# A two-layer decoder on one core: what is pinned behind a layer norm, the first pairs turned together, and other rates for the conditioning vectors

## The chip, the cores and the metric

The kernel runs on one core of a Trainium2 chip. The metric is the time of one execution on the device in microseconds. Before the change it is 2311.81 us, the median of three runs. A core has five engines that run side by side and wait for each other through semaphores: TensorE (PE, with its weight loads as PEld), VectorE (DVE), ScalarE (ACT), GpSimd (POOL) and SyncE (SP), which here issues the loads of weights.

## The reference

Two layers over 256 rows of width 2048, all in float32. Every sub-layer is `x <- LayerNorm(alpha * x + (1 + gate) * F(x * (1 + scale) + shift))`; shift, scale and gate come from a conditioning vector c through a 2048 x 12288 matrix per layer.

```python
c_act = silu(c)
for i in range(2):
    sh1, sc1, g1, sh2, sc2, g2 = split(c_act @ ada_w[i] + ada_b[i], 6)
    h = x * (1 + sc1) + sh1
    y = fox_attention(h) if i == 0 else swa_attention(h, positions)
    x = layer_norm(ALPHA * x + (1 + g1) * y)
    h = x * (1 + sc2) + sh2
    y = conv_ffn(h)                # up 2048 -> 2*5632, conv of width 3, silu gate, down
    x = layer_norm(ALPHA * x + (1 + g2) * y)
```

`fox_attention` has 16 heads of 128 with a forgetting term; `swa_attention` has 32 query heads of 64, 4 key/value heads, a window of 128, sinks and partial rotary.

## The kernel before

**Matrix products.** Everything is in float32 precision made of two parts: a value is split into a rounded high part (`h`) and a residual (`l`), and a product takes high x high, high x low and low x high. Weights come in tiles of 256 x 512 (`wtile`, 512 KB, ten buffers shared with the loads below). `stream` handles each tile: SyncE loads it (L265), ScalarE makes the high part (`wh`, L268), VectorE the residual (`wl`, L281), each with four buffers, and the function `go` runs the tile's matmuls: first all that need `wh`, then those that need `wl`. The modulated activations stand transposed in `hHL`, high and low parts, 16 chunks of 128 columns; a tile uses two chunks, called a pair here. `x_mm` keeps the rows of x as weights of TensorE (attention projections, down projections), `w_stationary` the weight tile (up projections of the FFN).

**Order of the work.** The program is written out in full by Python, and a planner then orders the instructions of each engine: by the order in which they were written, but an instruction that its model takes to be ready earlier may go ahead of one that is not. `pin` takes that freedom from an instruction: it is put behind the instruction written just before it on its engine. `work` is a queue of tiles (`go`) and small functions; `settle` runs it so that two tiles stay ahead, and `rest` writes the residuals (L281) of the next tiles before the current one runs, up to three in all. While `feeds` is not empty, `rest` writes only one.

**Layer norms.** There are three norms inside the program: behind the forgetting attention (near 489 us), behind the first FFN (near 1250 us) and behind the window attention (near 1543 us). The last `residual` adds the sub-layer to x and gathers statistics by halves of 128 rows (L573 to L587). A `halt` then calls `between`, which calls `modulate`. It runs ten matmuls on constants (`warm`), and eight feeds, one for each pair. A feed normalises a quarter of x where it begins one (`normalise`: rows 0 to 127 on ScalarE, L597; the others on VectorE, L599), transposes the pair on TensorE (`mod_turn`, L459), and applies scale and shift (`mod_pair`). The first two pairs take the fast form: for each chunk ScalarE writes the high part from PSUM (L469), VectorE computes the whole value from the same PSUM bank (L470) and subtracts (L471). The other six use L473 and L474 for a chunk each, then L85 and L86. Two feeds run at once, and each of the following six tiles runs one at its end. All of it is pinned, and so are the residuals of the tiles that were streamed while the halt was waiting or feeds were left.

**Conditioning vectors.** Ten of the twelve vectors are computed in the shadow of other work: `ada_vector` loads 32 parts of 512 KB, each with one VectorE operation (L396, the first of each half L394), and then needs some small matmuls and an evacuation, 37 steps in all. `ada_tick` runs after every tile: it adds `rate` to a debt and makes one step for each whole unit. `ada_need` makes what is missing at once where a vector is needed: the third norm needs the vectors that are written up to there. Functions put in `work` change the rate by stage. The first FFN has 96 and 80 tiles of up projections and 48 and 40 of down projections, in turn; the window attention 8 tiles for keys and values, 32 for queries, 32 for the output.

Of the kernel before, what the change touches and what calls it, by code (L numbers as in the profile page):

```python
# [17 lines left out]
P = 128  # L18
# [23 lines left out]
def hybrid_trunk(ctx: ExitStack, tc: tile.TileContext, a: dict, out: bass.AP):  # L42
# [23 lines left out]
    def bank(name="sm"):  # L66
        return psp.tile([P, 512], F32, tag="ps", name=name)
# [10 lines left out]
    def pin(ins, on=True):  # L78

        if on:  # L80
            tc.keep_in_program_order(ins)

    def split(h, l, src, on=False):

        pin(nc.scalar.copy(h, src), on)  # L85
        pin(nc.vector.tensor_tensor(l, src, f32(h), op=ALU.subtract), on)  # L86

    def split_v(h, l, src):
        nc.vector.tensor_copy(h, src)
# [134 lines left out]
    def rest(*items):  # L224

        n = 0
        for f in items:
            if f in stops:
                return
            if f in residuals:  # L230
                residuals[f]()
                n += 1
                if feeds:
                    return
            elif f in weights:
                n += 1
            if n > 2 - (items[0] not in weights):
                return
# [3 lines left out]
        stops.add(fn)  # L242
        then(fn)

    residuals, weights, stops = {}, set(), set()

    def defer(gen):

# [7 lines left out]
    def flush():  # L256
        while post:
            run_post()

    def stream(wsrc, row0, col, ks, use):  # L260

        for kc in ks[::2]:
            r0 = (row0 + kc) * P
            w = wtile()
            pin(nc.sync.dma_start(w, wsrc[r0:r0 + 2 * P, col:col + WB].rearrange("(k p) f -> p k f", p=P)), False)  # L265
            h = hl.tile([P, 2, WB], F32R, tag="wh", name="wh")
            l = hl.tile([P, 2, WB], F32R, tag="wl", name="wl")
            pin(nc.scalar.copy(h, w), False)  # L268

            def go(kc=kc, h=h, l=l):  # L270
                ahead[0] -= 1
                run_post()
                use(kc, h, l)
                if feeds:
                    feeds.pop(0)()
                tick()

            behind = bool(feeds) or any(f in stops for f in work)

            def residual_(w=w, h=h, l=l, go=go, behind=behind):  # L280
                pin(nc.vector.tensor_tensor(l, w, f32(h), op=ALU.subtract), behind or feeds)  # L281
                del residuals[go]

            ahead[0] += 1
            weights.add(go)
            residuals[go] = residual_
            work.append(go)
            settle(2)

    def x_mm(ps, kc, h, l, stat, last, first=0, ts=range(NT)):  # L290

        for t in ts:
            for i in range(2):
                xh, xl = stat(kc + i, t)
                mm(ps[t], xh, h[:, i, :], start=kc + i == first)
                mm(ps[t], xl, h[:, i, :])
        for t in ts:
            for i in range(2):
                mm(ps[t], stat(kc + i, t)[0], l[:, i, :], stop=kc + i == last)
# [33 lines left out]
    def w_stationary(wsrc, col):  # L333

        ps = [bank("wd") for _ in range(4)]

        def use(kc, h, l):
            cells = [(i, f) for i in range(2) for f in range(4)]
            for i, f in cells:
                mm(ps[f], h[:, i, f * P:(f + 1) * P], hHL[:, kc + i].rearrange("p a s -> p (a s)"),  # L340
                   start=kc + i == 0)
            for i, f in cells:
# [117 lines left out]
            os.append(o)  # L460
        return os

    def mod_pair(G, B, k, ps, fast=False, on=False):
        tmp = ttile()
        if fast:
            for j in range(2):
                o = tmp[:, j * S:(j + 1) * S]
                g, b = G[:, k + j:k + j + 1], B[:, k + j:k + j + 1]
                pin(nc.scalar.activation(hH[:, k + j, :], ps[j], AF.Identity, bias=b, scale=g))  # L469
                pin(nc.vector.tensor_scalar(o, ps[j], g, b, op0=ALU.mult, op1=ALU.add))  # L470
                pin(nc.vector.tensor_tensor(hL[:, k + j, :], o, f32(hH[:, k + j, :]), op=ALU.subtract))  # L471
            return
        pin(nc.scalar.activation(tmp[:, :S], ps[0], AF.Identity, bias=B[:, k:k + 1], scale=G[:, k:k + 1]), on)  # L473
        pin(nc.vector.tensor_scalar(tmp[:, S:], ps[1], G[:, k + 1:k + 2], B[:, k + 1:k + 2],  # L474
                                    op0=ALU.mult, op1=ALU.add), on)
        split(hH[:, k:k + 2, :], hL[:, k:k + 2, :], tmp.rearrange("p (j s) -> p j s", j=2), on)

    def hstat(kc, t):
        return hH[:, kc, t * P:(t + 1) * P], hL[:, kc, t * P:(t + 1) * P]
# [87 lines left out]
    moments = [None] * NT  # L567

    def residual(ps, d, gate, last):
        for t in range(NT):  # L570
            tmp = ttile()
            end = last and d == D // 512 - 1
            pin(nc.vector.tensor_tensor(tmp, ps[t], gate[:, d * 512:(d + 1) * 512], op=ALU.mult), end)  # L573
            xs = x[:, t, d * 512:(d + 1) * 512]
            pin(nc.vector.tensor_tensor(xs, xs, tmp, op=ALU.add), end)  # L575
            if last:
                pin(nc.vector.bn_stats(stats[:, t, d, :], xs), end)  # L577
                if d == D // 512 - 1:
                    mv = sp.tile([P, 2], F32, tag="mv", name="mv")
                    pin(nc.vector.bn_aggr(mv, stats[:, t].rearrange("p a b -> p (a b)")))  # L580
                    rs = sp.tile([P, 2], F32, tag="rs", name="rs")
                    pin(nc.vector.tensor_scalar_add(rs[:, 0:1], mv[:, 1:2], EPS))  # L582
                    if t == 0:
                        pin(nc.vector.tensor_scalar_mul(rs[:, 1:2], mv[:, 0:1], -1.0))
                    nc.gpsimd.tensor_tensor(rs[:, 0:1], rs[:, 0:1], mhalf, op=ALU.pow)
                    if t == 0:
                        nc.scalar.mul(rs[:, 1:2], rs[:, 1:2], rs[:, 0:1])  # L587
                    moments[t] = (mv[:, 0:1], rs[:, 0:1], rs[:, 1:2])
            yield

    def normalise(d):

        for t in range(NT):
            mu, rs, nm = moments[t]
            xs = x[:, t, d * 512:(d + 1) * 512]
            if t == 0:
                pin(nc.scalar.activation(xs, xs, AF.Identity, scale=rs, bias=nm))  # L597
            else:
                pin(nc.vector.tensor_scalar(xs, xs, mu, rs, op0=ALU.subtract, op1=ALU.mult))  # L599

# [86 lines left out]
    def out_proj(oT, full, w_o, l):  # L687
        def stat(kc, t):
            while kc not in full:
                step()  # L690
            return oT[kc][0][:, t * P:(t + 1) * P], oT[kc][1][:, t * P:(t + 1) * P]

        ps = {d: x_banks() for d in range(2)}

        def part(d, ks):
            use = x_mm_end(ps[d], stat, KC, 2) if d == D // WB - 1 else                 lambda kc, h, l_: x_mm(ps[d], kc, h, l_, stat, KC - 1)
            stream(w_o, 0, d * WB, ks, use)

        for i, ks in enumerate((range(0, 8), range(8, 12))):
            then(lambda i=i: ada.update(rate=((1.4,1.4,1.8,1.8), (1.05,)*4)[l][i]))  # L700
            for d in range(2):
                part(d, list(ks))
        then(lambda: ada_need(l, 2))
        for d in range(D // WB):
            if d < 2:
                part(d, list(range(12, KC)))
            else:
                then(lambda d=d: ada.update(rate=((1.4,1.4,1.8,1.8), (1.05,)*4)[l][d]))
# [202 lines left out]
    def swa(l, j):  # L911
# [94 lines left out]
    def conv_ffn(l):  # L1006
# [42 lines left out]
        for si, (b0, b1) in enumerate(sbs):  # L1049
# [79 lines left out]
```

## Time and profile before

| | |
|---|---|
| median of three runs | 2311.81 us |
| the profiled execution | 2310.31 us |
| its span, first to last instruction | 2308.4 us |
| TensorE busy | 2226.6 us, 96% of the span |
| VectorE busy | 1866.2 us, 81% |
| ScalarE busy | 1184.0 us, 51% |
| moved by DMA | 602.68 MB, mean 261 GB/s |
| L281, residuals of weights | 728 times, 1222 ns each |
| L396, conditioning vectors | 300 times, 1279 ns each |

A row of the timeline gives the start, the length, the engine, the line, the operation, what is written and read, how many were merged, and in square brackets how long the engine was idle before it and which instruction ended that. "xs", "wd" and "ws" are PSUM tiles of products, "sm" and "warm" small PSUM tiles. A row of busy time by stretch gives the busy time of each engine, the clock that TensorE was granted as a share of full speed, the busy share of the DMA engines and the bytes moved.

### The profile page before, as it was taken

What the parts mean: (1) busy time and instruction counts of PE and PEld (TensorE: products, weight loads), DVE (VectorE), ACT (ScalarE), POOL (GpSimd) and SP (SyncE); (2) the same over time, 40 slices, a digit from 0 to 9 for tenths busy, and PEclk for the clock granted to TensorE, in tenths of its full rate; (3) what the DMA queues carried; (4) which work ended last, traced back from release to release, by engine and by line L of the source; (5) the groups of instructions that cost most, each with busy time, mean ns of one, the idle gap of its engine ahead of it and who ended that gap; (6) DMA issues with size and microseconds to landing.
All of it is one profiled execution on the core that took longest, in us unless ns stands there. A gap on an engine that the chain in (4) does not pass through costs nothing. (4 is left out here: it accounts for less than half of the span.)

```text
span 2308.4 us, 33416 instructions
## 1 busy us (share of the span) xinstructions
PE 2226.6 (96%) x12225; PEld 1905.8 (83%) x12225; DVE 1866.2 (81%) x2783; ACT 1184.0 (51%) x1859; POOL 66.7 (3%) x83
## 2 busy tenths in 40 slices
PE   7889999999999999999999999998999999999997
PEld 7779898777888888888887777777888888888886
DVE  6898998969988886897986898888988754667666
ACT  3335644445655533555634478735665533555542
POOL 3230000000000000000000000000000000000000
PEclk9999999999999999999999999999999999999999
DMA  9998999958987897887896785787888556666553
GB/s 342 328 337 279 352 354 355 323 199 277 323 276 235 293 319 241 279 291 237 270 316 222 247 296 199 257 293 238 297 266 266 179 194 193 191 191 192 187 195 111
DMA packets 285989, 602.68 MB, mean 261 GB/s; under 512 B 20790, under 2 KB 53752, under 8 KB 285312
## 3 DMA queue, kind: packets, MB, share of 16 engines
q1 hardware_dynamic: 284768, 595.85, 76.9%
q0 software_dynamic: 1056, 4.69, 0.6%
q8 instruction: 96, 1.57, 0.3%
q14 instruction: 69, 0.57, 0.1%
HBM read 598.37 MB, written 2.10 MB: 260 GB/s over the span
## 5 line engine op out<-in xcount | busy, mean ns | idle before, releaser
L268 ACT CAST wh<-w 128x1024 fp32r<-128x1024 f32 x728 | 763.2, 1051 | 768.9 <-PE xs L76 263.5
L281 DVE TENSOR_TENSOR wl<-w,wh 128x1024 fp32r<-128x1024 f32 x728 | 887.7, 1222 | 306.3 <-ACT wh L268 285.5
L76 PE MATMUL wd<-hHL,wh 128*128 128x512 f32 x2816 | 720.3, 398 | 6.7 <-DVE hHL L86 3.3
L76 PEld LDWEIGHTS wd<-hHL,wh 128*128 128x128 f32 x2816 | 505.1, 189 | 108.3 <-DVE hHL L86 5.3
L76 PEld LDWEIGHTS wd<-hHL,wl 128*128 128x128 f32 x2816 | 374.3, 188 | 40.4 <-DVE wl L281 9.2
L76 PE MATMUL wd<-hHL,wl 128*128 128x256 f32 x2816 | 381.6, 278 | 6.3 <-DVE wl L281 6.2
L396 DVE SCALAR_TENSOR_TENSOR acc<-wa,cact,acc 128x1024 f32<-128x1024 f32 x300 | 380.7, 1279 | 0.0
L76 PE MATMUL xs<-wh,gT 128*128 128x512 f32 x1408 | 349.4, 389 | 0.0
L76 PEld LDWEIGHTS xs<-wh,gT 128*128 128x128 f32 x1408 | 263.6, 188 | 54.4
L76 PE MATMUL xs<-wl,gT 128*128 128x512 f32 x704 | 189.2, 389 | 0.0
L76 PE MATMUL xs<-wh,hHL 128*128 128x512 f32 x704 | 184.8, 399 | 3.4 <-DVE hHL L86 2.4
L76 PEld LDWEIGHTS xs<-wl,gT 128*128 128x128 f32 x704 | 132.1, 188 | 27.5
L76 PE MATMUL ws<-hHL,wh 128*128 128x256 f32 x1024 | 136.5, 287 | 16.1 <-ACT wh L268 16.1
L76 PEld LDWEIGHTS xs<-wh,hHL 128*128 128x128 f32 x704 | 127.8, 189 | 28.4 <-DVE hHL L86 2.7
L76 PEld LDWEIGHTS ws<-hHL,wh 128*128 128x128 f32 x1024 | 127.2, 193 | 21.9 <-ACT wh L268 21.3
L1019 ACT ACTIVATE u<-s,ccol 128x256 f32<-128x256 f32 x176 | 105.1, 600 | 65.0 <-DVE s L1014 50.3
L76 PE MATMUL xs<-wl,hHL 128*128 128x512 f32 x352 | 98.3, 399 | 4.1 <-DVE wl L281 4.1
L76 PE MATMUL xs<-wh,oT 128*128 128x512 f32 x384 | 99.1, 396 | 1.5 <-ACT wh L268 1.3
L528 DVE SCALAR_TENSOR_TENSOR oacc<-wo,cact,oacc 128x256 f32<-128x256 f32 x212 | 92.0, 494 | 6.2 <-POOL oacc L526 6.2
L1020 DVE SCALAR_TENSOR_TENSOR u<-s,ccol,u 128x255 f32<-128x255 f32 x176 | 84.4, 480 | 6.7 <-ACT u L1019 6.4
L1022 DVE SCALAR_TENSOR_TENSOR u<-s,ccol,u 128x254 f32<-128x254 f32 x176 | 84.1, 478 | 1.2
L76 PEld LDWEIGHTS xs<-wh,oT 128*128 128x128 f32 x384 | 70.7, 190 | 15.9 <-ACT wh L268 1.7
(218 smaller groups left out, 1705.3 us busy)
## 6 DMA issues: line engine op xcount, KB each, us to landing
w<-in_ffn_w_up_dram SPq DMA_DIRECT2D x352, 512.0 KB, 4.6
wa<-in_ada_w_dram SPq DMA_DIRECT2D x320, 512.0 KB, 4.9
w<-in_ffn_w_down_dram SPq DMA_DIRECT2D x176, 512.0 KB, 4.4
w<-in_fox_w_in_dram SPq DMA_DIRECT2D x96, 512.0 KB, 5.6
wo<-in_ada_w_dram SPq DMA_DIRECT2D x64, 512.0 KB, 6.4
w<-in_swa_w_in_dram SPq DMA_DIRECT2D x40, 512.0 KB, 4.8
w<-in_fox_w_o_dram SPq DMA_DIRECT2D x32, 512.0 KB, 6.0
w<-in_swa_w_o_dram SPq DMA_DIRECT2D x32, 512.0 KB, 5.6
```

The source lines that it names most:

```text
L76: return nc.tensor.matmul(o, lhsT, rhs, start=start, stop=stop, **kw)
L268: pin(nc.scalar.copy(h, w), False)
L281: pin(nc.vector.tensor_tensor(l, w, f32(h), op=ALU.subtract), behind or feeds)
L396: pin(nc.vector.scalar_tensor_tensor(ac, wo, cact[:, k:k + 1], ac, op0=ALU.mult, op1=ALU.add), True)
L528: nc.vector.scalar_tensor_tensor(acc[:, v, k % 2, :], w[:, k, :], cact[:, kc:kc + 1], acc[:, v, k % 2, :], op0=ALU.mult, op1=ALU.add)
L1019: nc.scalar.activation(u, s, AF.Identity, bias=cw(CW, f), scale=cw(2, f))
L1020: nc.vector.scalar_tensor_tensor(u[:, 1:], s[:, :S - 1], cw(1, f), u[:, 1:], op0=ALU.mult, op1=ALU.add)
L1022: nc.vector.scalar_tensor_tensor(u[:, 2:], s[:, :S - 2], cw(0, f), u[:, 2:], op0=ALU.mult, op1=ALU.add)
```

## The change

Six edits go together.

1. `mod_pair`: only the fast form's VectorE operations stay pinned. The other six pairs, ScalarE's part of `normalise` and ScalarE's L469 are left to the planner.
2. `rest` and `stream`: only the first two tiles streamed behind a halt have their residuals pinned and written one at a time (`behind`). Later tiles have them written up to three ahead, unpinned, while feeds are left.
3. `modulate`: the first quarter is normalised first; both first pairs are transposed together, all of rows 0 to 127, then six warming matmuls, then all of rows 128 to 255, then four. The warming matmuls stay twenty in all.
4. `mod_pair`, fast form: ScalarE takes chunk 0 while VectorE takes chunk 1, then the other way round; then the two subtractions.
5. `feed`: the next pair is turned in the middle of a tile, between the matmuls on `wh` and those on `wl`, not at its end.
6. Rates: window attention 1.25 to 0.95 (queries) and 1.05 to 0.9 (output); down projections of the first FFN 0.6 to 0.8.

In `residual` the same instructions are only written in another arrangement of the code.

```diff
     def rest(*items):
...
-                if feeds:
+                if f in behind:
                     return
...
+    fed = [False]
+
+    def feed():
+
+        if feeds and not fed[0]:
+            fed[0] = True
+            feeds.pop(0)()
...
                 run_post()
+                fed[0] = False
                 use(kc, h, l)
-                if feeds:
-                    feeds.pop(0)()
+                feed()
                 tick()
 
-            behind = bool(feeds) or any(f in stops for f in work)
-
-            def residual_(w=w, h=h, l=l, go=go, behind=behind):
-                pin(nc.vector.tensor_tensor(l, w, f32(h), op=ALU.subtract), behind or feeds)
+            def residual_(w=w, h=h, l=l, go=go):
+                pin(nc.vector.tensor_tensor(l, w, f32(h), op=ALU.subtract), go in behind)
                 del residuals[go]
 
+            if any(f in stops for f in work) and sum(f in behind for f in work) < 2:
+                behind.add(go)
...
                 mm(ps[t], xl, h[:, i, :])
+        feed()
         for t in ts:
...
-    def mod_pair(G, B, k, ps, fast=False, on=False):
+    def mod_pair(G, B, k, ps, fast=False):
         tmp = ttile()
         if fast:
+            g, b = ([c[:, k + j:k + j + 1] for j in range(2)] for c in (G, B))
+            o = [tmp[:, j * S:(j + 1) * S] for j in range(2)]
+            high = lambda j: nc.scalar.activation(hH[:, k + j, :], ps[j], AF.Identity, bias=b[j], scale=g[j])
+            whole = lambda j: pin(nc.vector.tensor_scalar(o[j], ps[j], g[j], b[j], op0=ALU.mult, op1=ALU.add))
+            high(0), whole(1), high(1), whole(0)
             for j in range(2):
-                o = tmp[:, j * S:(j + 1) * S]
-                g, b = G[:, k + j:k + j + 1], B[:, k + j:k + j + 1]
-                pin(nc.scalar.activation(hH[:, k + j, :], ps[j], AF.Identity, bias=b, scale=g))
-                pin(nc.vector.tensor_scalar(o, ps[j], g, b, op0=ALU.mult, op1=ALU.add))
-                pin(nc.vector.tensor_tensor(hL[:, k + j, :], o, f32(hH[:, k + j, :]), op=ALU.subtract))
+                pin(nc.vector.tensor_tensor(hL[:, k + j, :], o[j], f32(hH[:, k + j, :]), op=ALU.subtract))
             return
...
     def modulate(G, B, norm):
 
+        norm(0)
         warm(10)
-
-        def feed(k):
+        ps = {k: [bank() for _ in range(2)] for k in (0, 2)}
+        for t in range(NT):
+            for k in ps:
+                for j in range(2):
+                    pin(nc.tensor.transpose(ps[k][j][:, t * P:(t + 1) * P], x[:, t, (k + j) * P:(k + j + 1) * P], ident))
+            warm(6 - 2 * t)
+        for k in ps:
+            mod_pair(G, B, k, [b[:, :S] for b in ps[k]], True)
+
+        def feed_(k):
             if k % 4 == 0:
                 norm(k // 4)
-            o = mod_turn(k, 2)
-            if k < 4:
-                warm(5)
-            mod_pair(G, B, k, o, k < 4, True)
-
-        feeds.extend([lambda k=k: feed(k) for k in range(0, KC, 2)])
-        for _ in range(2):
-            feeds.pop(0)()
+            mod_pair(G, B, k, mod_turn(k, 2))
+
+        feeds.extend([lambda k=k: feed_(k) for k in range(4, KC, 2)])
...
     def normalise(d):
...
-                pin(nc.scalar.activation(xs, xs, AF.Identity, scale=rs, bias=nm))
+                nc.scalar.activation(xs, xs, AF.Identity, scale=rs, bias=nm)
...
-            then(lambda i=i: ada.update(rate=((1.4,1.4,1.8,1.8), (1.05,)*4)[l][i]))
+            then(lambda i=i: ada.update(rate=((1.4,1.4,1.8,1.8), (0.9,)*4)[l][i]))
...
-        then(lambda: ada.update(rate=1.25))
+        then(lambda: ada.update(rate=.95))
...
-                ada["rate"] = (0.6, 0.4)[l]
+                ada["rate"] = (0.8, 0.4)[l]
```

More of the change, by code (lines that the diff above doesn't have):

```diff
@@ L81, in pin, with split @@
             tc.keep_in_program_order(ins)
-    def split(h, l, src, on=False):
-        pin(nc.scalar.copy(h, src), on)
-        pin(nc.vector.tensor_tensor(l, src, f32(h), op=ALU.subtract), on)
+    def split(h, l, src):
+        nc.scalar.copy(h, src)
+        nc.vector.tensor_tensor(l, src, f32(h), op=ALU.subtract)
     def split_v(h, l, src):
@@ L243, in halt @@
         then(fn)
-    residuals, weights, stops = {}, set(), set()
+    residuals, weights, stops, behind = {}, set(), set(), set()
     def defer(gen):
@@ L341, in use @@
                    start=kc + i == 0)
+            feed()
             for i, f in cells:
@@ L569, in residual @@
     def residual(ps, d, gate, last):
+        c0 = d * 512
+        end = last and d == D // 512 - 1
         for t in range(NT):
             tmp = ttile()
-            end = last and d == D // 512 - 1
-            pin(nc.vector.tensor_tensor(tmp, ps[t], gate[:, d * 512:(d + 1) * 512], op=ALU.mult), end)
-            xs = x[:, t, d * 512:(d + 1) * 512]
+            xs = x[:, t, c0:c0 + 512]
+            pin(nc.vector.tensor_tensor(tmp, ps[t], gate[:, c0:c0 + 512], op=ALU.mult), end)
             pin(nc.vector.tensor_tensor(xs, xs, tmp, op=ALU.add), end)
@@ L577, in residual @@
                 pin(nc.vector.bn_stats(stats[:, t, d, :], xs), end)
[L578 to L588, printed above, removed]
+            if end:
+                mv = sp.tile([P, 2], F32, tag="mv", name="mv")
+                pin(nc.vector.bn_aggr(mv, stats[:, t].rearrange("p a b -> p (a b)")))
+                rs = sp.tile([P, 2], F32, tag="rs", name="rs")
+                pin(nc.vector.tensor_scalar_add(rs[:, 0:1], mv[:, 1:2], EPS))
+                if t == 0:
+                    pin(nc.vector.tensor_scalar_mul(rs[:, 1:2], mv[:, 0:1], -1.0))
+                nc.gpsimd.tensor_tensor(rs[:, 0:1], rs[:, 0:1], mhalf, op=ALU.pow)
+                if t == 0:
+                    nc.scalar.mul(rs[:, 1:2], rs[:, 1:2], rs[:, 0:1])
+                moments[t] = (mv[:, 0:1], rs[:, 0:1], rs[:, 1:2])
             yield
@@ L707, in out_proj @@
             else:
-                then(lambda d=d: ada.update(rate=((1.4,1.4,1.8,1.8), (1.05,)*4)[l][d]))
+                then(lambda d=d: ada.update(rate=((1.4,1.4,1.8,1.8), (0.9,)*4)[l][d]))
                 ps[d] = x_banks()
```

8 lines of the change are left out of this document (4 added, 4 removed).

## The prediction

> **What bounds the kernel now.** I read the page's busy times first, then busy time by stage, then the timeline behind the first layer norm, then who waited for whom.
>
> ```profile
> PE 2226.6 (96%) x12225; PEld 1905.8 (83%) x12225; DVE 1866.2 (81%) x2783; ACT 1184.0 (51%) x1859; POOL 66.7 (3%) x83
> ```
>
> TensorE is busy for 96% of 2308.4 us, so only its 82 us of idle time, plus matmuls that fill a wait, can be won. Columns below: stretch, its length, busy us of PE, PEld, DVE, ACT, POOL, granted clock, DMA share, GB/s.
>
> ```profile
> 0.00:170.00 170.00, 142.50 (x950) 129.90 (x950) 134.69 (x265) 60.16 (x76) 50.66 (x57) 0.99 0.99 336
> 498.50:521.00 22.50, 20.60 (x117) 17.03 (x118) 15.38 (x22) 12.48 (x18) 0.00 (x0) 1.00 0.61 187
> 521.00:561.00 40.00, 35.28 (x189) 29.16 (x188) 39.16 (x52) 21.20 (x30) 0.00 (x0) 0.96 0.83 275
> 552.00:555.00 3.00, 0.53 (x6) 0.34 (x4) 3.00 (x5) 1.27 (x4) 0.00 (x0) 0.93 0.87 289
> 555.00:559.00 4.00, 4.00 (x16) 3.59 (x17) 4.00 (x5) 0.99 (x1) 0.00 (x0) 0.63 1.00 348
> 770.00:900.00 130.00, 130.00 (x605) 108.58 (x604) 96.94 (x104) 53.42 (x60) 0.00 (x0) 1.00 0.81 281
> 1125.00:1246.00 121.00, 121.00 (x562) 101.08 (x561) 100.72 (x112) 52.12 (x59) 0.00 (x0) 1.00 0.87 303
> 1259.00:1283.00 24.00, 21.96 (x110) 17.15 (x109) 14.56 (x21) 14.14 (x20) 0.00 (x0) 1.00 0.41 119
> 1283.00:1400.00 117.00, 110.13 (x557) 88.87 (x556) 113.16 (x235) 75.44 (x174) 3.26 (x4) 1.00 0.82 282
> 1400.00:1538.00 138.00, 134.50 (x674) 109.95 (x673) 122.12 (x240) 91.78 (x217) 0.00 (x0) 1.00 0.75 261
> 1552.50:1575.00 22.50, 19.99 (x114) 16.34 (x114) 14.46 (x22) 13.25 (x19) 0.00 (x0) 1.00 0.58 184
> 1575.00:1616.00 41.00, 37.12 (x197) 31.03 (x198) 38.87 (x55) 20.34 (x31) 0.00 (x0) 0.96 0.81 261
> ```
>
> Three places lose time. While pairs are turned behind a norm (498.5, 1259, 1552.5) TensorE idles 1.90 + 2.04 + 2.51 = 6.45 us though VectorE is idle too (7.12, 9.44, 8.04 us): order, not work, is the limit. In the 40 us after that in each FFN, VectorE is full (39.16 of 40, 38.87 of 41) and TensorE idles 4.72 and 3.88 us. In the window attention's query projection VectorE is full again (113.16 of 117) and TensorE idles 6.87 us. The FFN's down projections (770, 1125) are the contrast: TensorE never idles and VectorE has 33.06 and 20.28 us free.
>
> **The gap at a norm.** The timeline behind the first norm:
>
> ```profile
> 488.30 0.63 PE L76 MATMUL xs<-wl,hHL 128*128 128x512 f32 x2
> 488.76 2.44 PE L76 MATMUL warm<-ones 128*128 128x512 f32 x10
> 492.89 0.44 PE L459 MATMUL sm<-ident,x 128*128 128x128 f32 x2 [1.48 <-DVE x L599]
> 493.26 1.02 ACT L469 ACTIVATE hHL<-sm,B,G 128x256 fp32r<-128x256 f32 x2 [2.58 <-PE sm L459]
> 493.86 0.55 DVE L470 TENSOR_SCALAR t<-sm,G,B 128x256 f32<-128x256 f32 x1 [1.02 <-ACT hHL L469]
> 494.44 0.42 DVE L471 TENSOR_TENSOR hHL<-t,hHL 128x256 fp32r<-128x256 f32 x1
> 495.92 2.02 PE L76 MATMUL wd<-hHL,wh 128*128 128x512 f32 x8
> 497.53 2.35 DVE L281 TENSOR_TENSOR wl<-w,wh 128x1024 fp32r<-128x1024 f32 x2
> 498.80 0.39 PE L76 MATMUL wd<-hHL,wl 128*128 128x256 f32 x1 [0.43 <-DVE wl L281]
> ```
>
> The last matmul ends at 488.93; the next useful one starts at 495.92. Up to 492.89 the path is the second half's statistics, which the change leaves alone. Then VectorE's L470 waits for ScalarE's L469 although both only read the same bank. With the engines on different banks VectorE starts with ScalarE at 493.26 instead of 493.86. Its eight operations are in order, so the first residual (497.53) and the matmuls on it (498.80) come 0.6 us earlier. The first matmul at 495.92 could come 0.97 earlier (493.26, two L470 of 0.55, an L471 of 0.42 and the handing over: the pair's first half is ready near 494.95), but the residual is late next, so I take 0.6 each, 1.8 for three; bounds 0.4 (six warming matmuls at 2.44 / 10 last 1.46 us and end just when the transposes are due) and 0.97.
>
> **Pairs in mid-tile, only the chain pinned.** Further on in the same stretch:
>
> ```profile
> 507.67 0.54 DVE L599 TENSOR_SCALAR x<-x,mv,rs 128x512 f32<-128x512 f32 x1
> 510.90 0.69 DVE L86 TENSOR_TENSOR hHL<-t,hHL 128x512 fp32r<-128x512 f32 x1 [1.60 <-ACT hHL L85]
> 511.64 2.13 PE L76 MATMUL wd<-hHL,wh 128*128 128x512 f32 x8 [0.91 <-DVE hHL L86]
> 517.05 1.05 ACT L268 CAST wh<-w 128x1024 fp32r<-128x1024 f32 x1 [3.16 <-DMA w<-in_ffn_w_up_dram]
> 554.96 2.08 PE L76 MATMUL wd<-hHL,wl 128*128 128x256 f32 x8 [2.47 <-DVE wl L281]
> ```
>
> A pair takes from 507.67 to 511.59 through VectorE, TensorE and ScalarE, and VectorE waits 1.60 us inside it because everything behind is pinned; TensorE waits for the pair at 511.64. Unpinned, VectorE can do a residual of 1.22 us in such a hole, and the pair starts half a tile earlier. No trace shows the new order, so the bounds are 0 and 6.45 us for the three stretches; I take half, 3.2, since part of the idle time is residuals and ScalarE.
>
> In the full stretches after it, VectorE's work is the same; only a head start helps, of up to the two more residuals that the lifted limit in `rest` allows. A residual is
>
> ```profile
> L281 DVE TENSOR_TENSOR wl<-w,wh 128x1024 fp32r<-128x1024 f32 x728 | 887.7, 1222 | 306.3 <-ACT wh L268 285.5
> L396 DVE SCALAR_TENSOR_TENSOR acc<-wa,cact,acc 128x1024 f32<-128x1024 f32 x300 | 380.7, 1279 | 0.0
> ```
>
> so 0 to 2.44 us for each FFN; I take one, 2.4 for both. The stall at 554.96 also costs clock: PE is busy 0.53 of 3 us, and the next 4 us are granted 0.63, so 4 x 0.37 + 3 x 0.07 = 1.7 us more are lost. The other FFN loses 41 x 0.04 = 1.6 the same way. I take one of the two as gone, 1.7; bounds 0 and 3.3. The Trainium skill (TensorE: Matmul & The Clock Gate, "HAM oscillation — how this bites in real kernels") has idle gaps over about 3.4 us as what throttles; by it the 2.47 us wait costs no clock and the whole sum would be 1.7 smaller. The trace disagrees, with 0.63 granted behind that wait.
>
> **The rates.** Each tile pays the rate into a debt; a vector takes 37 steps, 32 of them a load with one VectorE operation. Between the first norm and the third six vectors are due, 222 steps. The tiles are 176 up, 88 down, 8 key/value, 32 query, 32 output: before 176 x 0.52 + 88 x 0.6 + 8 x 0.3 + 32 x 1.25 + 32 x 1.05 = 220.3, so two steps are forced at the third norm; after 91.5 + 70.4 + 2.4 + 30.4 + 28.8 = 223.5, none. Running this count step by step, loads in the query projection go from 34 to 26, in the output projection from 30 to 22, in key/value from 0 to 2, in FFN0's down projections from 24 and 23 to 33 and 27, and one goes into an up projection. The trace bears the count out: between the second norm and the third it has
>
> ```profile
> L396 DVE SCALAR_TENSOR_TENSOR acc<-wa,cact,acc x60: 1260/1279/1287, 1301.0 to 1534.8; 128x1024 f32<-128x1024 f32 x60
> wa<-in_ada_w_dram SPq DMA_DIRECT2D x320, 512.0 KB, 4.9
> ```
>
> 60, which with two first rows for each of two vectors, written in another form, are the 34 + 30.
>
> The query projection loses 8 x 1.28 = 10.2 us of VectorE's 113.16. Its waits on TensorE's side:
>
> ```profile
> PE xs L76 <- DVE wl L281: 2.5, 4, 1.3
> PE qp L962 <- DVE qq L954: 2.5, 4, 1.1
> PE xs L76 <- ACT wh L268: 1.1, 1, 1.1
> ```
>
> 5.0 us are VectorE being late. I take 3.5, bounds 0 and 6.87: the wait at L962 is partly a chain's length. The output projection has VectorE at 122.12 of 138, not full: 0.5, bounds 0 and 3.50. FFN0's 13 more down loads I cost at nothing: 9 x 1.28 = 11.5 lies in 33.06 free, 4 x 1.28 = 5.1 in 20.28. DMA goes from 281 to 281 + 9 x 0.524 MB / 130 us = 317 GB/s, under the 336 at which the first row is full (0.99). Without that cover it is 13 x 1.28 = 16.6 us.
>
> One cover does go: the last vector's column sums sit in the third norm's gap.
>
> ```profile
> 1541.10 1.84 PE L76 MATMUL sm<-ones,acc 128*128 128x1 f32 x16
> 1542.80 2.56 PE L76 MATMUL warm<-ones 128*128 128x512 f32 x10
> ```
>
> Finished earlier, these 1.84 us stand between busy matmuls: +1.8, bounds 0 and 1.84.
>
> **Sum.** -1.8 - 3.2 - 2.4 - 1.7 - 3.5 - 0.5 + 1.8 = -11.3 us. The profiled execution took 2310.31 (2 us around its span), so 2299.0; the median shown is 2311.81, 1.5 more, which gives 2300.5. I say 2300.
>
> **Rivals.**
> - Only the arithmetic edits pay: the new order shifts TensorE's waits behind the norms without shortening them, since VectorE is full by 521 anyway. -1.8 - 3.5 - 0.5 + 1.8 = -4.0, so 2308. For it: 39.16 of 40. Against: 7 to 9 us of VectorE idle just before. 0.25.
> - All goes well: every stall behind the norms, both clock losses and the query projection's idle time vanish: -1.8 - 6.45 - 8.6 - 3.3 - 6.87 - 0.5 + 1.8 = -25.7, so 2286. Against it: some waits are chains and ScalarE's. 0.12.
> - Slower: an unpinned residual is placed ahead of a turned pair although its weights are late. At 517.05 a cast waits 3.16 us for its DMA; VectorE, in order behind it, would hold the pair, and TensorE with it, for 3.16 and a throttled window of 1.7. Once at each of the three norms is 14.6; with -4.0 from the other edits, +10.6, so 2322. It decides from about one such wait per norm; the old pins excluded it. Against it: SyncE issues the first seven tiles 10 us and more before the norm. 0.08.
>
> ```profile
> 460.19 8.69 SPq L265 DMA_DIRECT2D w<-in_ffn_w_up_dram  x4
> 471.98 2.10 SPq L265 DMA_DIRECT2D w<-in_ffn_w_up_dram  x2
> 477.17 0.37 SPq L265 DMA_DIRECT2D w<-in_ffn_w_up_dram  x1
> ```
>
> - FFN0's loads show after all: 16.6 - 11.3 = +5.3, 2317. 0.03.
> - The planner writes practically the old order and SWA waits on chains, not on VectorE: 2312. 0.07.
>
> **How the numbers follow.** The forecast has 0.45, and by its halves taken more or less it spreads over 2294 to 2306. The range 2287 to 2313 takes it, the first and the last rival and half of the second: about 0.83. A measurement of this kernel tells about 2% (46 us) from no change; no case reaches that, so 0.97 for within, 0.01 for faster, 0.02 for slower, where several mechanisms of delay would have to add up.
>
> **What would show it.** After the change: L470 should no longer wait for L469 and the first useful matmul come 6.0 to 6.5 us behind the last one, not 6.99. In the 22 us behind that, TensorE's idle time should halve and VectorE's fall; the granted clock in one of the two FFN stretches should be 1.00. The query projection's VectorE share should fall from 0.97 to about 0.88. FFN0's down projections should stay free of idle time at some 317 GB/s. The prediction is wrong if casts waiting for DMA appear ahead of turned pairs, or if the down projections idle.

## The result

The changed kernel takes 2278.9 us, the median of four runs between 2278.65 and 2279.10; the kernel before, beside it, 2309.7, the median of three runs (a fourth took 2804 us and is left out). The ratio is 0.9866 with a 95% interval of 0.9847 to 0.9886: 1.3% faster, about 31 us. That is within the 2% to which the prediction gave 0.97, but under the lower end of its range and under the most hopeful of its rivals.

The page of the changed kernel, its span and the engines' busy time:

```profile
span 2276.9 us, 33423 instructions
PE 2216.4 (97%) x12225; PEld 1902.6 (84%) x12225; DVE 1864.8 (82%) x2783; ACT 1183.8 (52%) x1859; POOL 63.8 (3%) x83
```

The instructions that compute are the same in number on each engine. TensorE's idle time falls from 81.8 to 60.5 us (span less busy), and its busy time by 10.2 us, of which the throttled stretches that are gone (40 and 41 us at 0.96) explain 3.2. By the stages of the table below, busy time falls by 3.7 and 3.6 us in the two up stages and by 5.7 in the query stage, and grows by 3.1 in FFN 1's rest; 2.9 us of this are 24 column sums that moved from the query stage into FFN 1's rest. What the remainder is made of was not taken apart. Line numbers have moved: L265 is L273, L268 L276, L281 L287, L469 L478, L470 L479.

Busy time by stretch of the changed kernel, in the order of the rows of before (the same stages, which now lie earlier; columns as there):

```profile
498.00:521.00 23.00, 22.59 (x134) 19.20 (x134) 22.77 (x31) 13.76 (x19) 0.00 (x0) 1.00 0.86 286
521.00:561.00 40.00, 40.00 (x235) 34.96 (x234) 39.52 (x59) 25.05 (x38) 0.00 (x0) 1.00 0.89 300
769.00:902.00 133.00, 133.00 (x606) 110.63 (x605) 109.70 (x114) 54.73 (x60) 0.00 (x0) 1.00 0.88 317
1130.00:1241.00 111.00, 111.00 (x506) 92.35 (x506) 94.01 (x106) 45.04 (x51) 0.00 (x0) 1.00 0.87 307
1250.00:1274.00 24.00, 22.24 (x105) 17.35 (x103) 22.66 (x30) 13.95 (x19) 0.00 (x0) 1.00 0.64 206
1274.00:1386.00 112.00, 109.60 (x559) 89.75 (x558) 100.89 (x226) 77.04 (x178) 1.14 (x4) 1.00 0.74 246
1386.00:1516.00 130.00, 128.81 (x660) 106.73 (x660) 112.70 (x230) 88.84 (x211) 0.00 (x0) 1.00 0.76 261
1529.50:1552.00 22.50, 21.55 (x131) 18.29 (x130) 22.02 (x29) 13.76 (x19) 0.00 (x0) 1.00 0.77 261
1552.00:1593.00 41.00, 41.00 (x238) 35.68 (x237) 41.00 (x63) 25.26 (x39) 0.00 (x0) 1.00 0.87 294
```

Behind the first norm VectorE is now busy 22.77 of 23 us, where it was 15.38 of 22.5, and DMA moves 286 GB/s instead of 187. In the 40 us after that VectorE is as full as before (39.52), but TensorE does not idle at all, and the clock is 1.00. The down projections (769, 1130) have no idle time either. The timeline behind the first norm:

```profile
492.94 1.48 ACT L478 ACTIVATE hHL<-sm,B,G 128x256 fp32r<-128x256 f32 x3 [0.47 <-PE sm L508]
493.05 1.03 DVE L479 TENSOR_SCALAR t<-sm,G,B 128x256 f32<-128x256 f32 x2 [0.53 <-PE sm L508]
494.68 2.10 PE L76 MATMUL wd<-hHL,wh 128*128 128x512 f32 x8 [0.53 <-DVE hHL L482]
496.49 2.35 DVE L287 TENSOR_TENSOR wl<-w,wh 128x1024 fp32r<-128x1024 f32 x2
497.77 1.21 PE L76 MATMUL wd<-hHL,wl 128*128 128x256 f32 x8 [0.55 <-DVE wl L287]
```

VectorE starts with ScalarE; the first product waits for the pair, and the first product on a residual still waits for the residual.

To see where the time went, the timelines of all kernels were cut at the same events. The first FFN, FFN0 in the prediction, is called FFN 1 here, the second FFN 2. "Gaps" is the sum of the three stretches from the start of the warming matmuls to the first product behind a norm; "FFN 1 up" and "FFN 2 up" go from that product to the first product of the down projections; "FFN 1 rest" from there to the warming matmuls; "query" from the first product of the window attention to the first of its output projection (keys and values included); "output" from there to the warming matmuls. What lies before the first norm, and behind the second FFN's first down product (the last product starts 461.04 us after it in every kernel), is left out.

| kernel | time, us | gaps | FFN 1 up | FFN 1 rest | query | output | FFN 2 up |
|---|---|---|---|---|---|---|---|
| before | 2309.7 | 21.3 | 284.0 | 469.6 | 165.7 | 120.4 | 283.9 |
| after | 2278.9 | 18.1 | 274.5 | 472.8 | 155.2 | 118.5 | 274.6 |
| e1 before + rates | 2314.2 | 21.5 | 282.8 | 472.8 | 164.7 | 118.4 | 284.9 |
| e2 before + pins and look-ahead | 2289.0 | 21.3 | 275.1 | 469.6 | 160.7 | 121.1 | 274.9 |
| e12 e2 + rates | 2282.9 | 21.5 | 275.1 | 472.8 | 155.1 | 118.4 | 275.1 |
| e3 after, old rates | 2284.7 | 18.1 | 274.5 | 469.6 | 161.3 | 120.6 | 274.5 |
| e4 after, pair turned at tile's end | 2281.6 | 18.1 | 275.3 | 472.8 | 155.9 | 118.4 | 275.3 |
| e5 after, one bank | 2280.9 | 18.1 | 275.2 | 472.8 | 155.8 | 118.4 | 275.3 |
| e6 after, pairs pinned | 2279.8 | 18.1 | 274.5 | 472.8 | 155.8 | 118.4 | 274.6 |
| e7 after, residuals pinned one by one | 2303.3 | 18.1 | 280.4 | 472.8 | 162.0 | 118.4 | 283.1 |
| e8 before + look-ahead, all pinned | 2307.0 | 21.3 | 281.4 | 469.6 | 166.8 | 120.2 | 280.6 |
| e10 after, residuals free, one by one | 2280.4 | 18.1 | 274.7 | 472.8 | 156.7 | 118.4 | 274.5 |
| e9 after, first residual early | 2277.4 | 18.1 | 274.2 | 472.8 | 153.2 | 118.4 | 274.3 |
| e11 e9 + sums in the gaps | 2276.0 | 19.7 | 274.2 | 472.8 | 155.0 | 118.4 | 274.2 |

The change takes 18.8 us from the two up stages, 10.5 from keys, values and queries, 1.9 from the output, 3.1 from the gaps, and puts 3.1 into FFN 1's rest. The kernel before ran beside each group of kernels, with medians of 2308.6 to 2310.4. So times from different groups can differ by 2 us without a cause in the kernel; the stages are those of one profiled execution of each kernel.

### The profile page after: what moved, and what is told of

It is laid out like the page before. It is cut to its first block, busy times and chain, and to the rows that moved or that the text cites. A ratio compares the mean times of both kernels' runs of the same rounds, so it can differ in the third digit from the quotient of the medians.

```text
span 2276.9 us, 33423 instructions
## 1 busy us (share of the span) xinstructions
PE 2216.4 (97%) x12225; PEld 1902.6 (84%) x12225; DVE 1864.8 (82%) x2783; ACT 1183.8 (52%) x1859; POOL 63.8 (3%) x83
## 5 line engine op out<-in xcount | busy, mean ns | idle before, releaser
L276 ACT CAST wh<-w 128x1024 fp32r<-128x1024 f32 x728 | 762.8, 1051 | 759.9 <-PE xs L76 285.8
L287 DVE TENSOR_TENSOR wl<-w,wh 128x1024 fp32r<-128x1024 f32 x728 | 886.3, 1220 | 299.6 <-ACT wh L276 270.2
L76 PEld LDWEIGHTS ws<-hHL,wh 128*128 128x128 f32 x1024 | 127.3, 194 | 21.8 <-ACT wh L276 21.3
```

The source lines that it names most:

```text
L76: return nc.tensor.matmul(o, lhsT, rhs, start=start, stop=stop, **kw)
```

## The experiments

**Which edit carries it.** Rates alone:

```diff
 before.py
-        then(lambda: ada.update(rate=1.25))
+        then(lambda: ada.update(rate=.95))
...
-(1.05,)*4   # twice
+(0.9,)*4
...
-                ada["rate"] = (0.6, 0.4)[l]
+                ada["rate"] = (0.8, 0.4)[l]
```

> Before with the new rates alone (edit 6). Stages before and after the whole change, read from the timelines: first FFN from its first product to its first down product 284.0 -> 274.5 us, the same of the second FFN 283.8 -> 274.6, window attention from its first product to the warming matmuls behind it 286.1 -> 273.7, the first FFN from its first down product to the warming matmuls behind it 469.7 -> 472.8. Theory 'order' (the 9 us in each FFN come from what is unpinned, the rates give only part of the window attention's 12): both FFN stages stay at 284, window attention falls to 278 to 282, the span by 2 to 5 us. Rival 'rates' (the loads carry it): window attention falls to 274 alone and the span by 9 or more, since the shifted sums put 3 us into the first FFN.

2314.2 us, ratio 1.0015 (1.0006 to 1.0025): slower, where 2 to 5 us less were expected. The FFN stages stay (282.8 and 284.9), FFN 1's rest grows by 3.1, the output gets 2.0 shorter and the query projection, with keys and values, only 1.0: 3.0 for the window attention, where 4 to 8 were expected. Theory "order" holds for the FFNs; that fewer loads help the query projection by themselves does not hold. The 24 column sums left that stage, but TensorE's idle time in it grew from 8.95 to 11.34 us. The profiled execution (2311.5) is the second fastest of ten, so not all of the loss of 3.8 us can be seen in these stages. The timeline of the query projection shows what it waits for:

```profile
1311.37 1.05 ACT L268 CAST wh<-w 128x1024 fp32r<-128x1024 f32 x1 [2.73 <-DMA w<-in_swa_w_in_dram]
1314.49 1.21 PE L76 MATMUL xs<-wl,hHL 128*128 128x512 f32 x4 [2.95 <-DVE wl L281]
```

The weights come late, the cast with them, then the residual, then TensorE. From 1259 to 1320 us TensorE's waits for residuals add up to 8.7 us, where they were 3.3 in the kernel before (e1 first):

```profile
PE xs L76 <- DVE wl L281: 8.7, 8, 2.9
```

```profile
PE xs L76 <- DVE wl L281: 3.3, 6, 1.3
```

Pins and look-ahead alone (in the fast form ScalarE's L469 stays pinned here):

```diff
 before.py
-                if feeds:
+                if f in behind:
                     return
...
-                pin(nc.vector.tensor_tensor(l, w, f32(h), op=ALU.subtract), behind or feeds)
+                pin(nc.vector.tensor_tensor(l, w, f32(h), op=ALU.subtract), go in behind)
...
-            mod_pair(G, B, k, o, k < 4, True)
+            mod_pair(G, B, k, o, k < 4)
...
-                pin(nc.scalar.activation(xs, xs, AF.Identity, scale=rs, bias=nm))
+                nc.scalar.activation(xs, xs, AF.Identity, scale=rs, bias=nm)
```

> Before with edits 1 and 2 alone (only the chain pinned, residuals up to three ahead). Theory 'order': VectorE fills its idle time behind the norms (15.4 of 22.5 us busy becomes over 20), so both FFN stages fall from 284 to 277 or less and the span falls by 14 us or more. Rival 'mid-tile' (pairs came too late because they were turned at a tile's end): FFN stages stay above 281 and the span falls by less than 6 us.

2289.0 us, ratio 0.9904 (0.9890 to 0.9919): two thirds of the gain. The FFN stages fall to 275. Its stretches, the 22.5 us in which pairs are turned and the 39.5 after:

```profile
500.00:522.50 22.50, 21.37 (x128) 18.45 (x129) 21.47 (x30) 14.06 (x19) 0.00 (x0) 1.00 0.83 267
522.50:562.00 39.50, 39.50 (x228) 34.17 (x227) 39.26 (x57) 23.64 (x36) 0.00 (x0) 1.00 0.89 301
```

VectorE is busy 21.47 of 22.5, and TensorE's idle time in the second stretch is gone. "Mid-tile" falls as the main cause. The rest of what it could be worth:

```diff
 after.py, in x_mm and w_stationary
-        feed()
```

> After with edit 5 undone: the next pair is turned at a tile's end again. Theory 'order': the planner moves the transposes by itself, so the time is within 3 us of after (2279). Rival 'mid-tile': FFN stages go back from 274.5 to 280 or more, the time to 2290 or more.

2281.6 us, within the 3 us that "order" allowed, but not nothing: 0.7 us in each of the three stages behind a norm.

**What of edits 1 and 2 counts.** Pairs pinned again, residuals free:

```diff
 after.py
-            mod_pair(G, B, k, mod_turn(k, 2))
+            mod_pair(G, B, k, mod_turn(k, 2), False, True)   # pins L484 to L487 and the copies of split
...
-                nc.scalar.activation(xs, xs, AF.Identity, scale=rs, bias=nm)
+                pin(nc.scalar.activation(xs, xs, AF.Identity, scale=rs, bias=nm))
```

> After with the six later pairs and ScalarE's part of the normalisation pinned again (edit 1 undone), the residuals still up to three ahead and free. Theory 'order' in its form 'holes in the pairs': VectorE has to wait inside each pair again, TensorE with it, FFN stages 278 to 282, time 2287 to 2297. In its form 'look-ahead': the residuals ahead are enough, FFN stages within 2 us of 274.5 and the time within 5 us of 2279.

2279.8 us; the stages are those of after, within 0.6 us. What this run undoes of edit 1 (all but the freedom of ScalarE's L478, the old L469) is worth about 1 us at most. Residuals pinned again, pairs free:

```diff
 after.py
-                if f in behind:
+                if feeds or f in behind:
                     return
...
-op=ALU.subtract), go in behind)
+op=ALU.subtract), go in behind or feeds)
```

> After with edit 2 undone: while feeds are left one residual at a time, pinned; the pairs stay free. Theory 'look-ahead' (the residuals written ahead are what fills VectorE behind a norm): both FFN stages go back from 274.5 to 281 or more, the query projection by 4 or more, the time to 2295 or more. Rival 'free pairs': FFN stages stay below 278, the time below 2287.

2303.3 us: most of the gain is gone (FFN stages 280.4 and 283.1, query 162.0; the first FFN a little under the 281 expected). Now only one half of edit 2, in the kernel before:

```diff
 before.py
-                if feeds:
+                if f in near:     # near: the first two tiles behind a halt
                     return
```

> Before with one line changed: the limit of one residual while feeds are left goes (up to three ahead, the first two behind a halt still one by one); everything stays pinned. Theory 'look-ahead': the number written ahead is what counts, so FFN stages fall from 284 to 277 or less, the span by 14 us or more. Rival 'freedom' (the planner must be allowed to move them): pinned residuals delay the pairs that stand behind them, FFN stages stay at 281 or more and the span falls by less than 6 us, or rises.

2307.0 us, ratio 0.9987 (0.9978 to 0.9997); the second FFN's 280.6 is a little under the 281 of "freedom". Written ahead but pinned, the residuals help little; about 1.7 us of each FFN's 2.6 and 3.3 can be the throttled window that does not occur here (in the first FFN the granted clock is 1.00, below). Busy time of e7 and e8, in this order, in the two stretches behind the first norm:

```profile
499.00:521.50 22.50, 21.48 (x125) 17.64 (x124) 17.01 (x24) 12.18 (x18) 0.00 (x0) 1.00 0.57 189
521.50:561.50 40.00, 36.01 (x209) 30.75 (x208) 39.91 (x56) 21.83 (x32) 0.00 (x0) 1.00 0.89 304
```

```profile
499.00:521.50 22.50, 20.09 (x114) 16.45 (x114) 15.57 (x23) 13.16 (x19) 0.00 (x0) 1.00 0.64 207
521.50:561.50 40.00, 36.47 (x206) 31.06 (x207) 40.00 (x56) 21.72 (x32) 0.00 (x0) 1.00 0.82 274
```

In both VectorE is idle for 5.5 to 7 us while pairs are turned, DMA moves about 200 GB/s, and TensorE idles 3.5 to 4 us afterwards. In e7 TensorE has little idle time in the first stretch (1.0 us), because the pairs come in time, and still pays in the second. Free but written one by one:

```diff
 after.py
-                if f in behind:
+                if feeds or f in behind:
                     return
```

> After, but while feeds are left the residuals are written one at a time; they stay free. With pinned residuals one at a time (the whole of edit 2 undone) the FFN stages were 280.4 and 283.1 and the time 2303, with pinned residuals up to three ahead in the kernel before 281.4 and 280.6. Theory 'freedom': the planner takes a free residual as soon as it is ready, wherever it was written, so FFN stages stay at 274.5 and the time within 3 us of 2279. Rival 'both': it needs them written ahead as well, FFN stages 277 or more, the time 2287 or more.

2280.4 us: "freedom". That the residual may move is what counts in the FFN stages, not how far ahead it is written; the query projection is 1.5 us longer. After with residuals pinned and up to three ahead was not run: e8 has them so, but in the kernel before.

**Why the rates help at all.** After with old rates, and e2 with the new ones:

> After with edit 6 undone (old rates). Alone, the new rates cost 3 us: 3.1 more in the first FFN, 3.0 less in the window attention. Theory 'only with a head start' (the loads taken from the query projection count only once VectorE is no longer behind from the norm): the query projection goes back from 155 to about 160 us, the output projection from 118.4 to 121, the first FFN's rest from 472.8 to 469.6, the time from 2279 to about 2284. Rival 'zero-sum' (what the window attention loses the first FFN gains): the time stays at 2276 to 2280.

> Before with edits 1, 2 and 6 (pins lifted, look-ahead, new rates), without the new turning of the pairs. Rates alone: +3.5 us on before. Pins alone: 2289.0. In after, the rates are worth 5.8 us (2284.7 to 2278.9). Theory 'interaction with the pins' (fewer loads help the query projection only where VectorE is not behind from the norm): 2282 to 2285, query projection 155 to 157 instead of 160.7. Rival 'interaction with the turning of the pairs' (edits 3 to 5): as alone, 2289 or more, query projection at 159 or more.

e3 is 2284.7, as the theory had it (query 161.3, output 120.6, FFN 1's rest 469.6). e12 is 2282.9, with 155.1 for the query projection. So by the medians the rates cost 3.8 us on the kernel before and win 6.1 on e2 and 5.8 on after, with e2 and e12, and e3 and after, in different groups. By the three stages that they change (FFN 1's rest, query, output) they cost 0.1 on the kernel before and win 5.2 on both others: they need the lifted pins, not the new turning. The 3.1 us in FFN 1's rest are mostly column sums. These groups of TensorE's instructions lie in that stage, first of before, then of after:

```profile
L76 PE MATMUL sm<-ones,acc 128*128 128x1 f32 x72 | 8.5, 240 | 0.0
```

```profile
L76 PE MATMUL sm<-ones,acc 128*128 128x1 f32 x96 | 11.4, 240 | 0.0
```

24 more, 2.9 us, in a stage where TensorE is never idle; the loads themselves show nowhere. The 24 come out of the query stage, so the two cancel.

**The first two pairs.**

```diff
 after.py
-            high(0), whole(1), high(1), whole(0)
             for j in range(2):
+                high(j), whole(j)
```

> After with edit 4 undone: in the first two pairs ScalarE and VectorE read the same bank one behind the other again. Theory 'bank': VectorE waits 0.5 to 0.6 us again at each of three norms, the gap from the warming matmuls to the first product goes from 6.25 to about 6.3 to 6.8 us and the first residual comes 0.6 later, so the time is 1 to 2 us over after (2279). Rival 'hidden': the gap is held by the chain before and the look-ahead takes the rest, the time stays within 0.6 us.

2280.9 us, 2.0 over after, though in another group. The gap stays 6.25: for the first product the rival "hidden" is right, while the first residual comes later, as "bank" had it:

```profile
493.15 0.55 DVE L479 TENSOR_SCALAR t<-sm,G,B 128x256 f32<-128x256 f32 x1 [1.02 <-ACT hHL L478]
498.10 1.07 PE L76 MATMUL wd<-hHL,wl 128*128 128x256 f32 x7 [1.26 <-DVE wl L287]
```

The wait of 1.02 us is back, TensorE waits 1.26 us for the residual instead of 0.55, and each of the three stages takes 0.6 to 0.7 us more. The shorter gaps themselves (21.3 to 18.1) are not the bank, since e5 keeps them, nor edits 5 and 6, since e4 and e3 keep them; e2 lacks them. What is left is the common turning of the pairs (edit 3) or ScalarE's freed L469, which were not tried apart.

**Versions that go further.** In after the residual is late next, and VectorE idles 6.78 us ahead of the norm. So:

```diff
 after.py
             if f in stops:
-                return
+                past = True
+                continue
             if f in residuals:
+                if past and f in second:    # second: the second tile behind a halt
+                    return
```

> After with the first tile's residual behind each norm made ahead of the norm's chain, where VectorE waits 6.78 us for the last product. In after TensorE waits 0.55 us for it (0.76 with the transposes' share). Theory 'the residual is late next': each norm gains 0.6 to 1.2 us, the time falls from 2279 to about 2276. Rival 'the pair is late next': the first product cannot start earlier and later waits take the gain, 2278 to 2279.

2277.4 us (2275.8 to 2278.8). The residual lies ahead of the norm, and the product on the first residual no longer waits:

```profile
480.55 1.22 DVE L290 TENSOR_TENSOR wl<-w,wh 128x1024 fp32r<-128x1024 f32 x1 [1.50 <-DMA w<-in_ffn_w_up_dram]
496.72 1.18 PE L76 MATMUL wd<-hHL,wl 128*128 128x256 f32 x8
```

The FFN stages gain 0.4 and 0.3, less than the 0.6 to 1.2 expected, the query projection 2.1. The slowest of the four runs is as slow as after, so the gain of 1.5 us is not sure. Then the last sums of the vectors due at the first and the third norm were left to the norm:

```diff
 e9
-((1.4,1.4,1.8,1.8), (0.9,)*4)   # twice
+((1.4,1.4,.62,.62), (0.78,)*4)
```

> The kernel with the first residual ahead of the norm (2277.4), and with rates at which the last 3 steps of the vector due at the first norm and the last 2 of the one due at the third are left to the norm (forgetting attention's last two blocks 1.8 to 0.62, window attention's output 0.9 to 0.78). Theory 'cover': 1.84 us of column sums each go back under the chain, where TensorE only warms, so the time falls by 2 to 4 us to about 2274. Rival 'chain': the vector's evacuation and what follows it delay the norm's own operations on VectorE, the gaps grow by as much and the time stays at 2277 or rises.

2276.0 us (2275.3 to 2276.5), ratio 0.9854 (0.9836 to 0.9872). Less than the 2 to 4 us expected: the warming matmuls now start at 484.25 instead of 488.38, but the first gap grows from 6.25 to 7.84, and the query projection loses 1.8 us again (153.2 to 155.0). The timeline of the gap, and the busy time of its first 5 us:

```profile
481.65 2.73 PE L76 MATMUL sm<-ones,acc 128*128 128x1 f32 x24
484.25 4.12 PE L76 MATMUL warm<-ones 128*128 128x512 f32 x10
```

```profile
484.00:489.00 5.00, 5.00 (x20) 4.03 (x20) 1.51 (x7) 2.63 (x4) 0.57 (x1) 0.66 0.59 210
```

TensorE is granted 0.66 there. Theory "cover" does not hold: from the end of the last product to the first product behind the norm it takes 10.27 us instead of 6.08 at the first norm, and 7.83 instead of 6.14 at the third, where 16 sums of 1.84 us came back. The warming matmuls and the transposes stand behind the sums in TensorE's order, so the sums push them back. What was won lies ahead of the first norm. There TensorE idled beside a full VectorE in e9, and does not in e11, where VectorE has three operations of the vectors less between 430 and 460 us. Busy time of e9, then of e11:

```profile
440.00:450.00 10.00, 8.66 (x39) 6.86 (x38) 10.00 (x12) 2.11 (x2) 0.00 (x0) 1.00 0.78 273
450.00:460.00 10.00, 8.37 (x44) 6.43 (x43) 10.00 (x10) 4.21 (x4) 0.00 (x0) 1.00 0.94 328
```

```profile
440.00:450.00 10.00, 10.00 (x45) 8.28 (x45) 10.00 (x12) 3.34 (x4) 0.00 (x0) 1.00 0.88 304
450.00:460.00 10.00, 10.00 (x45) 8.24 (x44) 10.00 (x10) 4.22 (x4) 0.00 (x0) 1.00 0.92 320
```

It is the lowest time of all; after's four runs and these four do not overlap, but the two did not run side by side, and the intervals of their ratios overlap.

## Why the prediction was wrong

The sign was right, the size was not: 11 us were forecast and 31 came.

**The full stretch behind the pairs is the step that failed.** It said that in the full stretches "VectorE's work is the same; only a head start helps, of up to the two more residuals", and took one for each FFN, 2.4 us for both, beside 3.2 for the pairs' own stretches and 1.7 of clock: 7.3. The two FFN stages alone gave 18.8. Of these, 11.5 are TensorE's idle time (6.75 and 6.67 us, now 0.96 and 0.95) and 3.2 the clock; 4 us of busy time were not taken apart. The full stretches' own idle time, 4.72 + 3.88 = 8.6 us, is gone altogether, where 2.4 were taken. The bound of two residuals came from the lifted limit in `rest`, and that limit is not what counts: with it lifted but the residuals pinned the FFN stages are 281.4 and 280.6 (e8), with it back but the residuals free 274.7 and 274.5 (e10). Two things were missed. First, the head start is larger: VectorE did 7 us more work in the 22 us in which pairs are turned, and that work was then not left for the full stretch. Residuals in this stretch, before and after:

```profile
L281 DVE TENSOR_TENSOR wl<-w,wh x6: 1217/1218/1221, 497.5 to 515.2; 128x1024 fp32r<-128x1024 f32 x6
```

```profile
L287 DVE TENSOR_TENSOR wl<-w,wh x9: 1216/1219/1222, 497.6 to 519.0; 128x1024 fp32r<-128x1024 f32 x9
```

22 us behind the start of the warming matmuls four tiles had their residual and TensorE had used four in the kernel before: no lead. After the change it is seven against four, a lead of three tiles where there are four buffers. Second, a residual done early frees its weight buffer, so that the next load starts early. Who ScalarE's casts waited for most, from 498 to 561 us, before, after and in e7:

```profile
ACT wh L268 <- DMA w<-in_ffn_w_up_dram: 11.4, 8, 3.2
```

```profile
ACT wh L276 <- PE wd L76: 18.5, 17, 2.0
```

```profile
ACT wh L276 <- PE wd L76: 9.8, 7, 3.5
ACT wh L276 <- DMA w<-in_ffn_w_up_dram: 6.5, 6, 2.5
```

Before, the casts waited 11.4 us for weights; after, they wait for none and mostly for buffers that TensorE still uses. With pinned residuals these waits for weights are 6.5 us (e7) and 8.5 (e8), with free ones 1.6 to 2.5 (e10, e6, e2). The prediction had quoted the 3.16 us wait of such a cast, but as the danger of the new order, not as the cost of the old one: the pins kept residuals, those kept the buffers, and those kept the loads. e6, e7 and e10 on the changed kernel, with e8 on the kernel before, show the cause of the gain in the FFN stages to be the residuals' freedom. That the earlier loads are part of the way is read from the rows above; it was not tried apart from VectorE's own lead.

**The gap.** The path was right for the residual: L470 no longer waits for L469, the bank is worth 0.6 to 0.7 us in the stage behind each norm (e5), and the residual is late next. It was wrong for the first product. That comes 6.08 us behind the last one at the first norm, inside the 6.0 to 6.5 forecast; counted from the warming matmuls it came 0.91, 1.58 and 0.66 us earlier at the three norms. But with the bank's wait back it comes as early (e5), so for the first product the prediction was right in size by luck, for the wrong edit, and the second norm's 1.58 was not foreseen. Edits 3 to 5 together are worth 4.0 us (e12 to after, in different groups).

**Half of the waits between pairs.** Of the 6.45 us 0.41 + 1.76 + 0.95 = 3.1 are left, about half, as forecast; half was only the middle of the bounds. The pairs' pins are not the reason: with them back (e6) the stages stay.

**Clock.** Both throttled windows behind the FFNs' stalls are gone, not one of two.

**The rates.** The count of steps was right: nothing is forced at the norm, FFN 1's down projections cover the loads, and DMA there is at 317 GB/s as worked out. TensorE's idle time in the query stretch fell from 6.87 to 2.40 us, 4.5 where 3.5 were taken. But the stage with keys and values lost 10.5: pins alone gave 5.0, and the 24 sums that left it 2.9. The term was put down as if the rates stood alone, where alone they win nothing (e1). VectorE's share there was read as too much work; it was also behind from the norm. Its waits in the changed kernel:

```profile
PE qp L978 <- DVE qq L970: 1.5, 3, 0.7
PE qp L978 <- ACT pT L688: 0.4, 1, 0.4
PE xs L76 <- DVE wl L287: 0.4, 1, 0.4
```

The wait for residuals fell from 2.5 to 0.4 us, that for the chain at L962 (now L978) from 2.5 to 1.5. VectorE's share fell to 100.89 of 112, 0.90, near the 0.88 forecast. The lost cover, +1.8, is a term that should not have been there, because the sums in the third norm's gap were hardly covered. From the end of the last product to the first behind that norm it takes 8.50 us with the 16 sums and 7.05 without (before and e1), and 7.83 and 6.14 with the new turning (e3 and after): at most 0.4 us of the 1.84 were hidden. The 3.1 us that FFN 1's rest grew by are the query stage's 24 sums, which cost as much there.

**The rivals.** "Only the arithmetic edits pay" falls: e2 without them has two thirds of the gain. "Slower" falls: no cast waits for DMA behind any of the three norms (498 to 561, 1247 to 1274, 1529.5 to 1593 us). FFN0's loads do not show, and the new order is not practically the old one. "All goes well" named the right stalls, and still gave too little, though 3.1 us between the pairs and 2.4 in the query stretch are left: it counted idle time and throttled stretches alone, while the busy rows shrank by 10.2 us, only 3.2 of them clock.

## What to carry to other kernels

When one engine is full and another waits for it, look at the time just before: work that an order pinned by hand kept out of idle time there is missing in the full stretch, and so, as the waits here suggest, are the buffers that it holds and the loads that need them. Pin only the chain that sets the end, and leave what merely runs ahead to move. Moving background work to a stage with room pays only if the stage that it leaves is limited by that work, and not by being behind; try such edits in both orders.

## What was not expected of the hardware

24 sums of one column took 2.73 us at the end of a stage, and the ten warming matmuls after them took 4.12 us instead of 2.44; TensorE counts as busy for 5.00 of 5 us there and was granted 0.66. A row of busy time does not say that the clock stays up. The 1.7 us are about what the first gap of e11 grew by (1.6). This was seen once: the 16 sums of 1.84 us ahead of the third norm of the same run are followed by ten warming matmuls in 2.56 us. That the sums are what lowered the clock was not tried.
